# Rotating images by 180 degrees on one core: a 2 KB strip in place of a 1 KB strip ahead of the first long store

## The chip, the cores and the metric

The kernel runs on one core of a Trainium2 chip. The metric is the device time of one execution in microseconds (us); the kernel before takes 122.12 us, the median of three runs (122.01, 122.12 and 122.31).

## The reference: what is computed

The input is 32 x 3 = 96 images of 256 x 256 float32. Each is turned by 180 degrees, so its 65,536 elements come out in reversed order. Nothing is calculated; 25.17 MB are read from HBM and 25.17 MB are written.

```python
def reference(x):
    return np.rot90(x, k=2, axes=(-2, -1)).astype(np.float32)
```

## The kernel before

**Tiling.** The 96 images are three groups of 32. An image is cut into four quarters, so that a group fills 128 partitions with one row of E = 16,384 elements (64 KB) each. The three groups have a buffer each in SBUF: `A`, `Bt` and `Ct`. To reverse an image, each quarter is reversed in its own row, in place, and the quarters change places: the store (L50) writes partition quarter 3 to quarter 0 of the image and so on, through the view `[:, ::-1, lo:hi]` of the output. A store of columns `lo:hi` therefore writes 128 contiguous pieces, one a row.

**Loads.** Three loads (L47), one for each group, are issued at the start: `A` and `Ct` from SP, which feeds the DMA queue called q1 in the profile, and `Bt` from ACT, which feeds q10. Each load is 128 rows of 64 KB. The memset of `Bt` (L62) puts a small wait ahead of the load of `Bt`. A DMA is shared out over 16 DMA engines, eight rows to each.

**Turning.** VectorE (DVE) does all of the reversing with copies (the helper `copy`, L44). `swap(t, lo, w)` exchanges `w` columns from the left of a row with the mirrored `w` columns from the right, both reversed, by three copies: right part into the scratch tile `T`, left part into the right part, `T` into the left part. `turn(t, lo, hi)` covers a stretch of the left half by swaps of at most J = 2048 columns; a whole buffer is `turn(t, 0, 8192)`, four swaps. The helper keeps these copies in program order.

**Order of the work.** After the load of `A`, DVE turns three of the four swaps of `A` (columns 0 to 6144 and their mirrors). The first of these swaps makes the columns 0 to 2047 final, and a first narrow store, here called the strip, sends columns 0 to `LEAD` = 256 of each row (1 KB a row, 128 KB in all). Then DVE turns `MID` = 2560 columns of `Bt` (a swap of 2048 and one of 512), and only then the fourth swap of `A`. That fourth swap releases the long store of `A`: columns 256 to 16,384 (63 KB a row), here called the long part. The rest of `Bt` follows (5632 columns in swaps of 2048, 2048 and 1536), its store, then `Ct` and its store. All stores are issued by SP, in this order, and so stand in q1 behind the loads of `A` and `Ct`.

The part of the code that sets this order:

```python
    turn(A, 0, half - J)
    store(A, 0, 0, LEAD)
    turn(Bt, 0, MID)
    turn(A, half - J, half)
    store(A, 0, LEAD, E)
    turn(Bt, MID, half)
    store(Bt, 1, 0, E)
```

Of the kernel before, what the change touches and what calls it, by code (L numbers as in the profile page):

```python
# [2 lines left out]

os.environ.setdefault("NEURON_RT_ULTRASERVER_MODE", "4")

# [4 lines left out]


@with_exitstack
def kernel(
    ctx: ExitStack,
    tc: tile.TileContext,
    x: bass.AP,
    out: bass.AP,
):
    nc = tc.nc  # L20
    P = 128

    B, C, H, W = x.shape
    L = H * W
    G = 32
    E = L // 4
    J = E // 8

    x4 = x.rearrange("b c h w -> (b c) (h w)").rearrange(
        "(g n) (s e) -> g (n s) e", n=G, s=4)  # L30
    o4 = out.rearrange("b c h w -> (b c) (h w)").rearrange(
        "(g n) (s e) -> g n s e", n=G, s=4)

    pool = ctx.enter_context(tc.tile_pool(name="slots", bufs=1))
    A = pool.tile([P, E], x.dtype, tag="A")
    Bt = pool.tile([P, E], x.dtype, tag="B")
    Ct = pool.tile([P, E], x.dtype, tag="C")
    T = pool.tile([P, J], x.dtype, tag="T")

    def back(t, lo, hi):  # L40
        return t[:, hi - 1:(lo - 1 if lo else None):-1]

    def copy(dst, src):
        tc.keep_in_program_order(nc.vector.tensor_copy(out=dst, in_=src))  # L44

    def load(t, g, lo, hi, queue=nc.sync):
        return queue.dma_start(out=t[:, lo:hi], in_=x4[g][:, lo:hi])  # L47

    def store(t, g, lo, hi):
        return nc.sync.dma_start(  # L50
            out=o4[g][:, ::-1, lo:hi], in_=t[:, lo:hi])

    def swap(t, lo, w):
        hi = E - lo - w
        copy(T[:, 0:w], back(t, hi, hi + w))
        copy(t[:, hi:hi + w], back(t, lo, lo + w))
        copy(t[:, lo:lo + w], T[:, 0:w])

    MID = 2560
    LEAD = 256  # L60
    load(A, 0, 0, E)
    nc.vector.memset(Bt[:, 0:256], 0.0)  # L62
    load(Bt, 1, 0, E, nc.scalar)
    load(Ct, 2, 0, E)

    def turn(t, lo, hi):
        while lo < hi:
            w = min(J, hi - lo)
            swap(t, lo, w)
            lo += w  # L70

    half = E // 2
# [7 lines that stand above are left out]
    turn(Ct, 0, half)  # L80
    store(Ct, 2, 0, E)


# [1 line left out]
_INS = ['x']  # L85
_OUTS = [((32, 3, 256, 256), 'float32')]


# [23 lines left out]
```

## Time and profile before

| what | value |
|---|---|
| median of the runs (lowest to highest) | 122.12 us (122.01 to 122.31) |
| the profiled execution, its own time | 122.04 us |
| its span, first to last instruction | 120.3 us |
| VectorE busy | 44.9 us (37%), 40 instructions |
| bytes moved, rate over the span | 50.33 MB, 419 GB/s |
| load of `A`: issue, until landed | 0.73 us, 38.8 us |
| load of `Bt` | 1.16 us, 43.2 us |
| load of `Ct` | 1.18 us, 60.2 us |
| strip of `A` (128 KB): issue, until landed | 43.33 us, 18.5 us |
| long part of `A` (8064 KB) | 59.85 us, 21.0 us |
| store of `Bt` | 70.40 us, 29.8 us |
| store of `Ct` | 85.54 us, 33.9 us |

Times inside the profile are microseconds from the start of the span. The profiled execution took 1.7 us more than its span, which lies around the first and last instruction. A transfer that is issued stands in its queue until each of the 16 DMA engines has come to it; the time until it has landed therefore holds the waiting as well. The profile records every packet of the DMA engines with its queue, size, start and duration; here a packet is one row's piece of a transfer (64 KB of a load, 1 KB of the strip, 63 KB of the long part) or a 4-byte completion. In the stretches of the windows view, a packet is counted, with all of its duration and bytes, in the stretch in which it starts, so that the DMA share of a short stretch can be over 1.

### The profile page before, as it was taken

The numbers are of one execution on the slowest core, as the hardware profiler recorded it, in microseconds if no ns is written. First come the engines' busy times: TensorE is split into PE (matmuls) and PEld (weight loads), VectorE is DVE, ScalarE is ACT, GpSimd is POOL, SyncE is SP. The second block draws the span as 40 slices with busy tenths as digits, with TensorE's granted clock in tenths as the row PEclk, the third lists the DMA queues.
The fourth block names the chain that finished last, engine by engine and source line by source line (L and its number), as shares of the span: only waits on it lengthen the run. The fifth ranks groups of instructions, "written<-read, shape, count | busy, mean of one in ns | idle before, by whom it ended". The sixth has DMA issues, their size and how long they took to land.

```text
span 120.3 us, 97 instructions
## 1 busy us (share of the span) xinstructions
DVE 44.9 (37%) x40; POOL 0.2 (0%) x4
## 2 busy tenths in 40 slices
DVE  0000000000000899999999999999400000000000
POOL 0000000000000000000000000000000000000000
DMA  9888988898889988998899977988898889888990
GB/s 349 349 349 371 676 349 349 349 676 371 349 349 632 414 349 349 632 414 349 349 387 622 408 343 343 687 349 349 349 698 349 349 349 676 371 349 349 654 392 0
DMA packets 1008, 50.33 MB, mean 419 GB/s; under 512 B 112, under 2 KB 240, under 8 KB 240
## 3 DMA queue, kind: packets, MB, share of 16 engines
q1 hardware_dynamic: 864, 41.94, 81.3%
q10 hardware_dynamic: 144, 8.39, 16.1%
HBM read 25.17 MB, written 25.17 MB: 419 GB/s over the span
## 4 chain that ended last, share of the span: by engine, by line
DVE 37%; DMA 32%; issue 1%
DMA A<-in_x_dram 32%; DVE T L44 12%; DVE Bt L44 9%; DVE A L44 8%; DVE Ct L44 8%
## 5 line engine op out<-in xcount | busy, mean ns | idle before, releaser
L44 DVE COPY T<-A 128x2048 f32<-128x2048 f32 x4 | 4.9, 1227 | 38.5 <-DMA A<-in_x_dram 38.4
L44 DVE COPY Bt<-Bt 128x2048 f32<-128x2048 f32 (+2 forms) x5 | 5.1, 1013 | 0.2
L44 DVE COPY T<-Bt 128x2048 f32<-128x2048 f32 (+2 forms) x5 | 5.1, 1013 | 0.2
L44 DVE COPY Bt<-T 128x2048 f32<-128x2048 f32 (+2 forms) x5 | 5.1, 1013 | 0.2
L44 DVE COPY A<-T 128x2048 f32<-128x2048 f32 x4 | 4.9, 1227 | 0.1
L44 DVE COPY A<-A 128x2048 f32<-128x2048 f32 x4 | 4.9, 1227 | 0.1
L44 DVE COPY T<-Ct 128x2048 f32<-128x2048 f32 x4 | 4.9, 1227 | 0.1
L44 DVE COPY Ct<-T 128x2048 f32<-128x2048 f32 x4 | 4.9, 1227 | 0.1
L44 DVE COPY Ct<-Ct 128x2048 f32<-128x2048 f32 x4 | 4.9, 1226 | 0.1
L62 DVE MEMSET Bt<- 128x256 f32 x1 | 0.3, 272 | 0.9 <-PEq L96 0.9
L96 POOL MEMSET const-bfloat16-1.0<- 128x1 bf16 x1 | 0.1, 103 | 0.0
L96 POOL MEMSET const-uint8-127<- 128x1 uint8 x1 | 0.1, 102 | 0.0
L96 POOL MEMSET const-float32-0.0<- 128x1 f32 x1 | 0.1, 99 | 0.2 <-issue 0.2
L96 POOL MEMSET const-float32-1.0<- 128x1 f32 x1 | 0.1, 99 | 0.0
## 6 DMA issues: line engine op xcount, KB each, us to landing
out_dram<-A SPq DMA_DIRECT2D x1, 8064.0 KB, 21.0
out_dram<-A SPq DMA_DIRECT2D x1, 128.0 KB, 18.5
A<-in_x_dram SPq DMA_DIRECT2D x1, 38.8
Bt<-in_x_dram ACTq DMA_DIRECT2D x1, 43.2
Ct<-in_x_dram SPq DMA_DIRECT2D x1, 60.2
out_dram<-Bt SPq DMA_DIRECT2D x1, 29.8
out_dram<-Ct SPq DMA_DIRECT2D x1, 33.9
```

The lines of the kernel that those rows point to most:

```text
L44: tc.keep_in_program_order(nc.vector.tensor_copy(out=dst, in_=src))
L62: nc.vector.memset(Bt[:, 0:256], 0.0)
L96: nc = _bacc.Bacc("TRN2", target_bir_lowering=False, num_devices=1)
```

## The change

Two constants change. The strip becomes 512 columns (2 KB a row, 256 KB in all) and the long part begins at column 512 (62 KB a row). `Bt` is turned for 2432 columns, not 2560, ahead of the fourth swap of `A`: its second swap is 384 columns wide in place of 512. After the long part is issued, 5760 columns of `Bt` are left, in swaps of 2048, 2048 and 1664. The number, kind and order of the instructions on each engine stay as they were: VectorE has three copies of 384 columns in place of three of 512, and three of 1664 in place of three of 1536; SP issues the same seven transfers, two of them with another width.

```diff
-    MID = 2560
-    LEAD = 256
+    MID = 2432
+    LEAD = 512
```

## The prediction

> **What bounds the kernel.** I read the page first: span, engines, DMA packets, queues.
>
> ```profile
> span 120.3 us, 97 instructions
> ...
> DVE 44.9 (37%) x40; POOL 0.2 (0%) x4
> ...
> DMA packets 1008, 50.33 MB, mean 419 GB/s; under 512 B 112, under 2 KB 240, under 8 KB 240
> ...
> q1 hardware_dynamic: 864, 41.94, 81.3%
> q10 hardware_dynamic: 144, 8.39, 16.1%
> ```
>
> VectorE is busy for 37% of the span. The packets of the two queues together took 97.4% of the time of 16 DMA engines, which is 117.2 us for each. By the packet records the first packets start at 1.75 to 2.41 us (mean 1.93) and the last end at 118.89 to 119.13 us (mean 119.03): 117.1 us lie between. So, but for some tenths of a microsecond, the DMA engines never stop. The kernel is bound by moving 50.33 MB, and a change of order can only win what the engines lose on the way.
>
> Next the queue's own waits on SP, then the timeline around the change.
>
> ```profile
> SPq L50 <- DVE A L44: 19.6, 2, 15.9
> SPq L107 <- DMA out_dram<-Ct: 19.3, 1, 19.3
> ```
>
> ```profile
> 58.60 1.23 DVE L44 COPY A<-T 128x2048 f32<-128x2048 f32 x1
> 59.85 0.54 SPq L50 DMA_DIRECT2D out_dram<-A  x1
> 59.86 1.23 DVE L44 COPY T<-Bt 128x2048 f32<-128x2048 f32 x1
> ```
>
> The end (L107) waits for the store of `Ct`, which was issued at 85.54 us and landed 33.9 us later: it stood in its queue. The one store that is issued close to the moment at which it is needed is the long part of `A`, at 59.85 us, just as the load of `Ct` runs out. Only there can the change act. So I cut the span into stretches at the starts of the rows (columns: length, VectorE, POOL, clock, DMA share, GB/s).
>
> ```profile
> 55.46:57.88 2.42, 2.32 (x4) 0.00 (x0) 1.00 1.00 433
> 57.88:60.30 2.42, 2.35 (x3) 0.00 (x0) 1.00 1.06 433
> 60.30:60.81 0.51, 0.51 (x1) 0.00 (x0) 1.00 0.33 115
> 60.81:61.05 0.24, 0.24 (x1) 0.00 (x0) 1.00 0.49 162
> 61.05:61.20 0.15, 0.12 (x2) 0.00 (x0) 1.00 10.44 4424
> 61.20:61.48 0.28, 0.28 (x1) 0.00 (x0) 1.00 3.35 1437
> ```
>
> The first stretch holds the 16 packets of the last but one row of `Ct`: share 1.00, 2.42 us each. The second holds the 16 packets of its last row: 6% longer, 2.57 us on the mean. The strip follows. No row of the long part starts before 61.05; then 4424 GB/s for 0.15 us is 664 KB, ten rows of 64,512 bytes and some strip packets, and the last stretch holds the other six rows. Ten engines starting together means that they had waited for the transfer to arrive, 1.2 us after its issue. The packet records, put together engine by engine, say it exactly (us; lengthening is against 2.42):
>
> ```
> engines      last Ct row ends  lengthened by  strip ends     long part starts  idle
> first ten    60.45 to 60.68    0.00 to 0.20   60.80 to 61.02  61.06 to 61.14   0.11 to 0.26
> other six    60.87 to 61.13    0.17 to 0.27   61.21 to 61.47  61.22 to 61.48   0.00
> ```
>
> The strip takes 0.34 us on an engine, eight packets 0.043 us apart. Ten engines idle; six go from strip to long part at once, and these are the last. The order holds to the end: the engine that starts the long part last, at 61.476, runs its rows in 2.380 us each (later 2.418) without a pause and ends at 119.13, last of all. I call it the **pacing engine**. The earlier ones run rows of 2.380 to 2.39 and close up: the spread of 0.38 us after the first long row is 0.24 at the end.
>
> **The change, part by part.**
>
> *The strip.* A 1 KB packet costs 0.0425 us; at the rate of the long rows (64,512 bytes in 2.380 us, 27.1 bytes a ns) its bytes are 0.0378, so 0.0047 is the packet's own cost. A 2 KB packet is then 0.0756 + 0.0047 = 0.080, and eight are 0.64 us, +0.30 on each engine. Bounds: 0.60 if the own cost goes, 0.68 if it doubles with the size. I take 0.64, since only the bytes grow.
>
> *The long part.* Its rows are 1,024 bytes shorter: 8 x 0.0378 = -0.30 us on each engine. With the strip that is 0.00 on the pacing engine (bounds -0.04 and +0.04).
>
> *The swaps of `Bt`.* A copy of 512 columns takes 0.427 us, of 1536 0.960: 0.52 ns a column. A 384-column copy is then 0.360. Three of them save 3 x 0.067 = 0.20 us ahead of the fourth swap of `A`, so the long part is issued at 59.65 and reaches the engines at 60.86. The three copies of 1664 columns cost 1.027 each, +0.20, so the store of `Bt` is issued at 70.40 as before. It is needed at 80.15, when the first engine ends its long rows: 9.7 us of cover. `Ct`'s store has 99.5 - 85.5 = 14 us. The strip's issue on SP (43.33) stays; SP has nothing else before 59.65. No wait is added.
>
> *The idle time.* The first engine will now end its strip at 60.455 + 0.64 = 61.10, and the long part is there at 60.86. All ten idle stretches go, 1.56 us in sum, 0.10 us on the mean over 16 engines, and perhaps the 0.04 us by which the first long row was longer on these ten (2.42 against 2.38). The wider strip alone just covers it (61.10 against 61.06); the narrower swap gives 0.2 us of margin. But it is the engines ahead of the pacing engine that gain. The pacing engine had no idle time: 0.00.
>
> *The last row of `Ct`.* It is longer by up to 0.27 us where the load meets the strip, by 0.24 on the pacing engine (2.660). The next longest rows where one transfer meets another are 2.433 (long part to `Bt`), so this belongs to the passage from load to store. Nothing in the trace tells how it grows with the size of the strip. Bounds: it goes (-0.24), or it doubles with the strip's bytes (+0.24); and since the long part now arrives at 60.86, before six engines have ended their last `Ct` row, it may add as much again (+0.48). I take 0.00, the value of the one row there is.
>
> **Sum:** 0.00 on the pacing engine, so 122.04 for the profiled execution, which is 0.08 below the median of the runs, and 122.1 for the median. Everything that the pacing engine loses after its first row is 0.24 and 8 x 0.0047 = 0.04: no reordering here can win more than about 0.3 us, unless the engines share their rate.
>
> **The rivals.**
>
> *The store crowds the end of the load (slower).* If the lengthening of the last `Ct` row comes from store bytes that already stand in the queue, the change puts twice as many there, and the long part before the loads have ended. For it: the lengthening is only there, the strip was queued from 43.9 us on, and 0.27 is near the 0.30 us that 8 KB take on an engine. Against it: three engines, with the same strip behind them, had rows lengthened by under 0.01. Price: strip alone +0.24, 122.4; with the long part as well +0.48, 122.6. It decides, beyond what a measurement tells, once the pacing engine's last `Ct` row is over 0.61 us longer (now 0.24). The Trainium skill speaks on this side: the page "DMA: Bandwidth & Descriptors", section "Two DMAs through the same engine are not ordered", says that a queue's transfers are pipelined in an engine, whose read and write sides are separate. By that rule the strip can be read while the load is still being written, so that what is queued early need not wait its turn; the lengthened rows do not contradict it, and no run here shows the two sides apart.
>
> *The engines share a rate.* The early engines close up from 0.38 to 0.24 us, as if they gave way. If all of the idle time counted for the total, 0.10 to 0.13 us would be won: 122.0. If the issue of the long part set the end, 0.20 us would come straight off: 121.9. Against both: the pacing engine runs at the shortest row time, 2.380, throughout.
>
> *All gains at once (faster).* The lengthening vanishes (-0.24) and the shared idle time comes on top (-0.13): 121.7. Nothing supports both together.
>
> **How the numbers follow.** A measurement of this kernel tells about 0.3% from no change, 0.37 us. The forecast, nothing on the pacing engine, 122.1: 0.50. The strip alone crowds the load, 122.4: 0.13. Strip and long part crowd it, 122.6: 0.21. Shared rate or issue, 121.9 to 122.0: 0.09. All gains, 121.7: 0.07. So faster by over 0.3% 0.07, within 0.3% 0.50 + 0.13 + 0.09 = 0.72, slower 0.21. The range leaves out the last gain and the upper half of the crowding: 121.8 to 122.6.
>
> **What would show it.** In the profile after, the long part should be issued at about 59.65; the first engines should start it at about 61.10, each right behind its strip, spread over some 0.6 us instead of ten at once; the strip should take 0.64 us on an engine; and the stretch of `Ct`'s last row should keep a share of about 1.06. A share near 1.12 or above speaks for crowding, 1.00 for the lost lengthening. The last packets should end near 119.1, with a spread wider than 0.24, as the early engines win what the last one does not. The forecast is wrong if the last engine to start the long part is more than 0.3 us later or earlier, counted without the strip's 0.30, than 61.48, or if long rows change from 27.1 bytes a ns.

## The result, and the profile after

The changed kernel takes 122.27 us (median of 22 runs, 122.06 to 122.67), the kernel before 122.04 us beside it (22 runs). The ratio is 1.0022, with a 95% interval of 1.0014 to 1.0029: slower by 0.22%, some 0.25 us. The profiled execution took 122.29 us with a span of 120.5, against 122.04 and 120.3.

The page of the kernel after: as much work of VectorE, as many packets, and the strip's 128 packets are no longer under 2 KB.

```profile
span 120.5 us, 97 instructions
...
DVE 44.9 (37%) x40; POOL 0.2 (0%) x4
...
DMA packets 1008, 50.33 MB, mean 418 GB/s; under 512 B 112, under 2 KB 112, under 8 KB 240
```

The timeline of the kernel after shows the 384-column copies and the sooner issue of the long part.

```profile
55.02 0.36 DVE L44 COPY Bt<-Bt 128x384 f32<-128x384 f32 x1
...
58.33 1.23 DVE L44 COPY A<-T 128x2048 f32<-128x2048 f32 x1
59.58 0.55 SPq L50 DMA_DIRECT2D out_dram<-A  x1
```

Here are the stretches of the kernel after, cut at its own starts of rows (columns: length, VectorE, POOL, clock, DMA share, GB/s).

```profile
55.59:58.01 2.42, 2.35 (x3) 0.00 (x0) 1.00 1.00 433
58.01:60.43 2.42, 2.35 (x3) 0.00 (x0) 1.00 1.13 433
60.74:61.38 0.64, 0.61 (x2) 0.00 (x0) 1.00 0.79 301
61.38:61.60 0.22, 0.22 (x1) 0.00 (x0) 1.00 7.94 3407
61.60:62.02 0.42, 0.42 (x1) 0.00 (x0) 1.00 1.86 800
63.72:66.06 2.34, 2.27 (x3) 0.00 (x0) 1.00 1.00 434
```

The first two hold the same two rows of `Ct` as the pair shown for the kernel before. The last but one row is the same, 1.00. The last row has gone from 1.06 to 1.13: its 16 packets take 2.73 us on the mean, against 2.56. The next stretch has strip packets alone. The long part starts between 61.38 and 62.02, eleven rows in the fourth stretch (3407 GB/s for 0.22 us is 750 KB) and five in the fifth, as each engine comes to the end of its strip; nothing is idle. The prediction had named this share as its sign: 1.12 or above for crowding, 1.00 for a lengthening that is lost. The packet records carry no number of the engine; packets are joined into 16 chains where one starts within 0.01 us of the end of another, and across idle time in the order of time. This is the chain of the pacing engine in both kernels:

```
pacing engine            before    after     difference
last Ct row starts       58.469    58.453    -0.02
it takes                  2.660     2.912    +0.25
strip, with completion    0.347     0.648    +0.30
long part starts         61.476    62.013    +0.54
8 long rows of            2.380     2.342    -0.30
last packet ends        119.134   119.371    +0.24
```

The whole difference, 0.24 us at the last packet and 0.25 in the time, is the last row of `Ct`. Strip and long rows cancel.

### The profile page after: what moved, and what is told of

It reads as the page before. It is cut to its first block, busy times and chain, and to the rows that moved or that the text cites. A ratio compares the mean times of both kernels' runs of the same rounds, so it can differ in the third digit from the quotient of the medians.

```text
span 120.5 us, 97 instructions
## 1 busy us (share of the span) xinstructions
DVE 44.9 (37%) x40; POOL 0.2 (0%) x4
## 4 chain that ended last, share of the span: by engine, by line
DVE 37%; DMA 32%; issue 1%
DMA A<-in_x_dram 32%; DVE T L44 12%; DVE Bt L44 9%; DVE A L44 8%; DVE Ct L44 8%
## 6 DMA issues: line engine op xcount, KB each, us to landing
out_dram<-A SPq DMA_DIRECT2D x1, 256.0 KB, 19.1
```

## The experiments

The theory: **bytes that a later transfer is to read from SBUF, standing in the queue behind the load of `Ct`, lengthen the load's last row.** The expectations call it Q where they speak of store bytes, and R where they add that these are read from SBUF ahead of their turn. Rivals: the sooner long part does it (L), the passage from load to store does it whatever is queued (P), the width of the strip costs by itself, the writes to HBM do it (W), or any further transfer does (S). The table has one line for each run. "Row" is the mean packet of the last `Ct` row (without lengthening it is 2.418 to 2.422), "long" the start of the long part, or of the whole store of `A`, on the last engine, "end" the end of the last packet; these are of one profiled execution each. Ratios are to the kernel before, with 95% intervals.

```
strip, columns of Bt         ratio                     row    long    end
1 KB, 2560 (before)          1                         2.557  61.48  119.13
the same, profiled again     one time, 121.97 us       2.517  61.39  119.06
2 KB, 2432 (after)           1.0022 [1.0014, 1.0029]   2.733  62.01  119.37
2 KB, 2560                   1.0021 [1.0005, 1.0037]   2.856  61.97  119.33
2 KB, 2560, moved in code    1.0037 [1.0022, 1.0052]   2.838  62.06  119.42
1 KB, 2432                   0.9994 [0.9980, 1.0007]   2.460  61.28  118.94
1 KB, 2432, again            0.9987 [0.9975, 1.0000]   2.459  61.26  118.92
none, 2560                   1.0030 [1.0020, 1.0040]   2.418  61.42  119.59
8 KB, 2560                   1.0066 [1.0047, 1.0085]   3.633  64.73  120.28
load in its place, 2560      1.0039 [1.0024, 1.0054]   2.440  61.56  119.52
copy in SBUF, 2560           1.0077 [1.0055, 1.0099]   2.696  62.29  120.25
none, 0                      1.0081 [1.0063, 1.0099]   3.324  61.96  119.92
2 KB issued after, 2560      1.0034 [1.0022, 1.0045]   2.421  61.95  119.52
none, 2304                   1.0004 [0.9995, 1.0014]   2.420  61.15  119.34
1 KB, 2304                   0.9988 [0.9976, 0.9999]   2.496  61.33  118.98
512 B, 2304                  0.9989 [0.9980, 0.9999]   2.443  61.12  119.03
2 KB, 2304                   1.0026 [1.0010, 1.0041]   2.740  61.85  119.21
```

### The change taken apart

The wider strip alone:

```diff
-    LEAD = 256
+    LEAD = 512
```

> The strip is 2 KB a row, the first part of Bt stays at 2560 columns. Theory Q (store bytes that already stand in the queue behind the load of Ct lengthen its last row, in proportion to their number): the mean packet of the last Ct row is about 2.75 us, as in the changed kernel (2.42 without lengthening, 2.57 with the 1 KB strip), and the time is 0.2 to 0.3 us above the kernel before. Theory L (the long part, arriving 0.2 us sooner, lengthens the row): the mean packet stays at 2.57 us and the time within 0.05 us of the kernel before.

```profile
57.80:60.22 2.42, 2.35 (x3) 0.00 (x0) 1.00 1.18 433
```

Slower by 0.21%, row 2.856, a share of 1.18 (1.06 in the kernel before). The strip alone brings the whole loss. The row was expected at 2.75; it is 0.1 us longer than that.

The narrower swap alone:

```diff
-    MID = 2560
+    MID = 2432
```

> The strip stays at 1 KB a row, 2432 columns of Bt are turned ahead of the fourth swap of A, so that the long part is issued at 59.65 us. Theory Q: the last Ct row keeps a mean packet of 2.57 us, the idle stretches of the ten early engines shrink by 0.2 us each, and the time stays within 0.05 us of the kernel before, since the last engine had none. Theory L: mean packet about 2.75 us and 0.2 to 0.3 us slower.

```profile
57.80:60.22 2.42, 2.35 (x3) 0.00 (x0) 1.00 1.02 433
```

The ratio of 0.9994 leaves no loss to it, and the row is not longer but a little shorter. Theory L falls. The pacing engine gained, though it had no idle time: its last row was 2.432 against 2.660.

### How the last row depends on the strip

No strip (the first `store` call is taken out):

```diff
-    LEAD = 256
+    LEAD = 0
...
-    store(A, 0, 0, LEAD)
```

> No strip: the whole store of A (64 KB a row) is issued where the long part was, at 59.85 us. Theory Q: the last Ct row is not lengthened at all, its mean packet is 2.42 us; the engines end it at about 60.3 to 60.9 and idle until the store arrives at 61.06, start together, and the time is within 0.1 us of the kernel before, since what is won on the row is lost in the wait. A third theory, P (the lengthening belongs to the passage from load to store, whatever is queued): 2.57 us for the packet again, and the time within 0.1 us too.

With nothing behind the load the row is 2.418 on the mean, and no engine is over 2.420. P falls. The stretches of this kernel:

```profile
57.97:60.39 2.42, 2.35 (x3) 0.00 (x0) 1.00 1.00 433
60.39:61.25 0.86, 0.84 (x1) 0.00 (x0) 1.00 0.01 0
61.25:61.45 0.20, 0.18 (x1) 0.00 (x0) 1.00 12.27 5243
```

The last `Ct` row has a share of 1.00; then nothing but completions starts until 61.25, and all 16 rows of the store start within 0.2 us. The time missed the expectation: 0.30% above, not within 0.1 us. The last engine ended its `Ct` row at 61.06 and waited 0.35 us. And the 24 rows that followed took it 58.17 us, against 57.96 for the same 24 rows in the kernel with no strip and no columns of `Bt`, whose engines start between 61.29 and 61.96. The expectation had set the wait equal to the 0.24 us won on the row, and had left out the slower rows.

A strip of 8 KB:

```diff
-    LEAD = 256
+    LEAD = 2048
```

> The strip is 2048 columns, 8 KB a row, 64 KB on each engine, eight times that of the kernel before. Theory Q without a limit: the last Ct row of the last engine is 8 x 0.24 = 1.9 us longer than 2.42, and the kernel 1.7 us slower than before. Theory Q with a limit to what an engine takes up ahead: more than the 0.49 us of the 2 KB strip, less than 1.9 us, and the time above before by that less 0.24 us. Theory L: 0.24 us as before, and the same time.

```profile
57.80:60.22 2.42, 2.35 (x3) 0.00 (x0) 1.00 1.50 433
```

That stretch of the 8 KB kernel has a share of 1.50: row 3.633, on the last engine 3.598, 1.18 us longer. That is far from eight times 0.24; the growth is not in proportion.

The whole store queued early (strip taken out, and the fourth swap of `A` ahead of all of `Bt`):

```diff
-    MID = 2560
-    LEAD = 256
+    MID = 0
+    LEAD = 0
...
-    store(A, 0, 0, LEAD)
```

> No strip, and no part of Bt is turned ahead of the fourth swap of A: the whole store of A, 64 KB a row, is issued at about 54.7 us and stands in the queue when the load of Ct ends. Theory Q, by the 8 KB strip (64 KB on each engine, mean row 3.63 us): the last Ct row takes 3.6 us or more, no engine idles, and the time is about 0.9 us above the kernel before. If only packets of a strip, of 8 KB and less, do it, the row stays at 2.42 us, the stores follow at once, and the time is 0.2 to 0.3 us below the kernel before.

```profile
57.80:60.22 2.42, 2.35 (x3) 0.00 (x0) 1.00 1.37 433
```

The store was issued at 54.64 us and stood in the queue; the row took 3.324 on the mean (up to 3.70), and the kernel is 0.81% slower with no engine idle. A packet of 64 KB does it as well as small ones. The row is shorter than behind the 8 KB strip, though 3.6 us or more was expected and eight times as many bytes stood in the queue when the row began, so the lengthening has a limit. The run also shows what the work order of the kernel before is good for: it keeps the long part out of the queue until the loads end.

### Width, or standing in the queue

First the strip was moved in the code behind the fourth swap, with 512 columns:

```diff
-    store(A, 0, 0, LEAD)
     turn(Bt, 0, MID)
     turn(A, half - J, half)
+    store(A, 0, 0, LEAD)
     store(A, 0, LEAD, E)
```

> The 2 KB strip is issued by SP only with the long part, at 59.85 us, in place of 43.3 us, so that it reaches the DMA engines (1.2 us later, 61.06) after the load of Ct has ended. Theory Q (store bytes that stand in the queue behind the load lengthen its last row): the last Ct row goes back to 2.42 us with the same strip, the last engine starts its long part at about 61.06 + 0.64 = 61.7 us against 62.01 in the changed kernel, and the time is within 0.1 us of the kernel before, 0.2 to 0.3 us below the changed one. Rival, the width of the strip by itself (2 KB packets) costs: the time stays 0.2 to 0.3 us above the kernel before.

This did not do what it was meant to: the timeline has the strip on SP at 43.39 us as ever (the line below takes the first two stores of `A` together), since it waits only for the columns that it reads, and these are final after the first swap. So it is a second look at the 2 KB strip with 2560 columns (row 2.838), and says nothing on the rival.

```profile
43.39 17.07 SPq L50 DMA_DIRECT2D out_dram<-A  x2
```

Then the first swap of `A` itself was put last:

```diff
-    LEAD = 256
+    LEAD = 512
...
-    turn(A, 0, half - J)
-    store(A, 0, 0, LEAD)
+    turn(A, J, half)
     turn(Bt, 0, MID)
-    turn(A, half - J, half)
+    turn(A, 0, J)
+    store(A, 0, 0, LEAD)
     store(A, 0, LEAD, E)
```

> The first swap of A is turned last, after the 2560 columns of Bt, so that the 2 KB strip cannot be issued before 59.85 us, together with the long part, and reaches the DMA engines at about 61.06, after the load of Ct has ended. Theory R (store bytes in the queue behind the load are read from SBUF ahead of their turn and lengthen its last row): the last Ct row takes 2.42 us, though the strip is as wide as in the changed kernel; the last engine starts its long part at about 61.75 us against 62.01, and the time is 0.2 to 0.3 us below the changed kernel, within 0.1 us of the kernel before. Rival, the wider strip costs by its width alone: 0.2 us or more above the kernel before, with a last Ct row of 2.7 us.

Now the timeline has both stores on SP, one after the other, from 59.83 us, and the stretch of the last row is clean:

```profile
59.83 1.27 SPq L50 DMA_DIRECT2D out_dram<-A  x2
```

```profile
57.80:60.22 2.42, 2.35 (x3) 0.00 (x0) 1.00 1.00 433
```

The same 2 KB strip no longer lengthens the row (2.421, at most 2.449). Width is not the cause; standing in the queue behind the load is. The time did not fall with it: 0.34% above, where 0.0 was expected. The first strip packet starts at 61.115, 1.28 us after the issue, while the last engine had ended its load at 60.92; it starts its long part at 61.95, and the rows from there to the end take 57.57 us against 57.36 in the changed kernel. What the row won, the wait and the slower rows gave back.

### What kind of transfer does it

A load of the same size in the strip's place, into an unused tile, with `LEAD = 0`:

```diff
+    U = pool.tile([P, 512], x.dtype, tag="U")
...
-    store(A, 0, 0, LEAD)
+    nc.sync.dma_start(out=U, in_=x4[0][:, 0:512])
```

> The store strip is replaced by a load of the same size (2 KB of each row of the input into an unused tile), queued behind the load of Ct; the whole store of A is issued at 59.85 us. It moves 0.26 MB more than the kernel before. Theory R (the engine reads the strip from SBUF ahead of its turn, while it still writes the last load row into SBUF) and theory W (writes of the strip to HBM meet the last reads from HBM): the last Ct row stays at 2.42 us, the extra load takes 0.64 us on an engine, the last one starts its store at about 61.55, and the time is about 0.35 us above the kernel before. Theory S (any further transfer in the queue lengthens the row): 2.73 us or more for that row, and 0.6 to 0.8 us above.

```profile
57.80:60.22 2.42, 2.35 (x3) 0.00 (x0) 1.00 1.01 433
```

Row 2.440: three engines took 2.51 to 2.56, the others 2.418 to 2.420. The kernel is 0.39% slower, 0.47 us, where about 0.35 was expected for the extra 0.26 MB. A further transfer as such does not lengthen the row to 2.73; S falls.

A copy of the strip's columns from SBUF to SBUF, again with `LEAD = 0`:

```diff
+    U = pool.tile([P, 512], x.dtype, tag="U")
...
-    store(A, 0, 0, LEAD)
+    nc.sync.dma_start(out=U, in_=A[:, 0:512])
```

> The store strip is replaced by a copy of the same columns from A in SBUF to an unused tile in SBUF, issued where the strip was; the whole store of A is issued at 59.85 us. It moves 0.26 MB more inside SBUF. Theory R: the last Ct row is lengthened as by the 2 KB strip, to a mean of 2.7 to 2.9 us, though nothing is written to HBM, and the time is 0.6 to 0.9 us above the kernel before. Theory W: 2.42 us for the row, since the copy writes nothing to HBM, and about 0.35 us above.

```profile
57.80:60.22 2.42, 2.35 (x3) 0.00 (x0) 1.00 1.11 433
```

The copy writes nothing to HBM, and the row is lengthened all the same: 2.696, on every engine by 0.09 us or more, at most to 2.906. W is not needed. Load and copy both write 2 KB a row into SBUF from the same place in the queue; only the copy reads it from SBUF. The ratio is 1.0077 against 1.0039. So, between these two, the lengthening comes with the queued read of SBUF. One difference is left in the pair: the extra load waits for nothing and was issued at once, the copy when the first swap had ended. The pages give the time from issue to landing, 60.3 and 19.1 us:

```profile
U<-in_x_dram SPq DMA_DIRECT2D x1, 256.0 KB, 60.3
...
U<-A SPq DMA_DIRECT2D x1, 256.0 KB, 19.1
```

A load that is issued as late as the copy was not run. Of the 0.73 us by which the last packets of the two executions differ, 0.49 is the last row on the last engine; the rest is that this row began 0.24 us later.

The traces bound the theory in two ways. In the changed kernel the store of `Bt`, which also reads SBUF, is issued 9.8 us before the first engine ends its long rows, yet the eighth long row takes 2.342 us on every engine like the seven before it: behind this store there is no lengthening. And in the kernel with the extra load, the last engine writes its 2 KB rows from 60.92 to 61.56 us, while the store reaches the first engines at 61.12; these packets take 0.084 us throughout. So what was seen is the lengthening of a 64 KB load row; for short packets, behind which the store has only just come, none was seen.

### The sooner long part, and a better version

> The kernel before, profiled once more, to see how far the lengthening of the last Ct row differs from one execution to the next. Expected: a mean packet of 2.50 to 2.62 us (2.56 at first), the first ten or so engines idle for 0.1 to 0.25 us ahead of the long part, and 122.0 us.

Row 2.517, 121.97 us; here thirteen engines idle ahead of the long part, for 0.02 to 0.14 us, and again the last three do not. Expected were about ten engines with 0.1 to 0.25 us.

> The same kernel as the narrower swap alone (strip 1 KB, 2432 columns), run again, for its time and for a second look at the last Ct row. If the mean packet of 2.46 us, against 2.56 in the kernel before, comes from the sooner arrival of the long part, it stays near 2.46 and the time 0.1 us below the kernel before; if it was chance, it lies anywhere between 2.45 and 2.65, and the time is within 0.05 us of the kernel before.

Row 2.459 again, ratio 0.9987 with an interval that just reaches 1.

Four kernels with `MID = 2304` followed, with no strip and with strips of 1 KB, 512 bytes and 2 KB:

```diff
-    MID = 2560
-    LEAD = 256
+    MID = 2304
+    LEAD = 0
...
-    store(A, 0, 0, LEAD)
```

> No strip, and 2304 columns of Bt ahead of the fourth swap of A: the whole store of A is issued at about 59.45 us and reaches the engines at 60.66, while the last rows of Ct end at 60.3 to 60.9. Theory R: early engines idle for at most 0.3 us, the last ones have a row lengthened by at most some tenths, and the time is 0.2 to 0.4 us below that of the kernel with no strip and 2560 columns, so about that of the kernel before (0.0 to 0.1 us above). Were the wait for the store not the cost there, the time would stay 0.4 us above the kernel before.

As expected: 0.33 us less than with no strip and 2560 columns (122.13 against 122.46), with the row still at 2.420. The wait for the store was most of the cost there: on the last engine it went from 0.35 to 0.10 us.

```diff
-    MID = 2560
+    MID = 2304
```

> The strip of the kernel before (1 KB) and 2304 columns of Bt, so that the long part is issued 0.40 us sooner than before, at about 59.45 us, and reaches the engines at 60.66, while most last rows of Ct (60.4 to 61.0) are still being written. If the sooner long part shortens the last Ct row (2.46 us on the mean at 2432 columns in both looks, 2.52 and 2.56 at 2560), it is 2.40 to 2.46 here and the time 0.1 to 0.2 us below the kernel before. If store bytes in the queue lengthen it, as theory R says, the long part's bytes now do, the mean is over 2.6 us, and the time 0.0 to 0.3 us above the kernel before.

```diff
-    MID = 2560
-    LEAD = 256
+    MID = 2304
+    LEAD = 128
```

> A strip of 512 bytes a row, and 2304 columns of Bt (long part at about 59.45 us). Theory R: the strip alone would lengthen the last Ct row by some 0.07 us on the mean (0.14 with 1 KB), the strip takes about 0.19 us on an engine, so most engines end it near the 60.66 us at which the long part arrives; the time is 0.1 to 0.2 us below the kernel before, as with the 1 KB strip and 2432 columns. If the wait for the long part or its bytes cost more than that, the time is at or above that of the kernel before.

```diff
-    MID = 2560
-    LEAD = 256
+    MID = 2304
+    LEAD = 512
```

> The changed kernel with 2304 columns of Bt in place of 2432: the 2 KB strip and a long part issued at about 59.45 us. If the sooner long part shortens the last Ct row also behind a 2 KB strip (2.73 us at 2432 columns, 2.84 and 2.86 at 2560), it is about 2.6 us here and the time 0.1 us below the changed kernel. If it does not (no reason is known why it should), the mean is 2.7 us or more and the time that of the changed kernel or 0.1 us above it.

With the 1 KB strip the row is 2.50, ratio 0.9988; with 512 bytes 2.44, ratio 0.9989; with 2 KB 2.74, 0.26% slower. With 1 KB that is neither of the two rows expected (2.40 to 2.46, or over 2.6). The sooner issue goes along with a shorter row by 0.06 to 0.12 us between 2560 and 2432 columns, in one or two profiled executions each, for both widths of strip (2.46, 2.46 against 2.52, 2.56; 2.73 against 2.84, 2.86), and a further 128 columns bring nothing more (2.50; 2.74). Why a sooner long part should shorten the row is not settled: the theory would have it longer. The best versions are the kernel before with 2432 or 2304 columns, about 0.1 us faster (121.9 against 122.05), at the edge of what the runs can tell.

## Why the prediction was wrong

**Right.** *The bound*: the DMA engines stay busy, and only the passage from load to store changed. *The pacing engine*: the engine that starts the long part last ended last in both kernels, and the end moved with it (+0.54 at the start of the long part, -0.30 in its rows, +0.24 at the end). *The strip*: forecast 0.64 us, measured 0.644 (0.648 with its completion). *The long part*: rows of 2.342 us, as forecast. *The swaps*: copies of 0.360 us as forecast, long part issued at 59.58 (59.65 forecast; this execution's first store was 0.07 sooner as well), `Bt`'s store at 70.33 with its cover whole. *The idle time*: all ten idle stretches are gone, and the pacing engine, which had none, won nothing by it. The spread of the last packets is 0.62 us, wider than 0.24, as forecast.

**Wrong, one step: "The last row of `Ct`" - "I take 0.00, the value of the one row there is."** It was +0.25 us on the pacing engine (2.660 to 2.912) and +0.18 on the mean. The first engine started its long part at 61.39 instead of 61.10: 0.16 us of that is its longer last row, and 0.13 that this row began later in this execution. The bound set beside it, +0.24 if it doubles with the strip's bytes, is what came; the rival "The store crowds the end of the load" had the mechanism, and its price for the strip alone, +0.24 us, the loss. It had been put behind for three engines whose rows were not lengthened. That was one look at something that differs from engine to engine and from look to look: behind a 1 KB strip the pacing engine's row was longer by 0.24, 0.01, 0.22, 0.29 and 0.01 us in five executions, behind 2 KB by 0.49, 0.58, 0.55 and 0.51 in four. Three rows out of 16 that escape do not speak against a cause which acts on the mean. That the pacing engine's row doubled so exactly is therefore partly luck. The second half of the rival's price (0.24 more from the long part) did not come: the narrower swap cost nothing.

The doubling is not a law either. The mean lengthening was 0.02 us with 512 bytes a row, 0.04 to 0.14 with 1 KB, 0.31 to 0.44 with 2 KB, 1.21 with 8 KB, 0.91 with a queued 64 KB row. The Trainium skill, page "DMA: Bandwidth & Descriptors", section "Two DMAs through the same engine are not ordered", has the read and the write side of an engine as separate queues. The pair of load and copy agrees with a read side that takes up the next transfer's SBUF reads while the row is still being written (2.440 against 2.696); that it happens inside the engine, and not on the way to SBUF, no run here shows.

The +0.22% lies within the range given for the time, but the forecast was no change, and the rival that the numbers follow had been given 0.13. The prediction's limit for being wrong, 0.3 us at the start of the last engine's long part, was too wide to notice: without the strip's 0.30 that start moved by 0.24.

## What to carry to other kernels

Where a load and a store follow each other in one DMA queue, do not queue more of the store behind the load than is needed to bridge the time until the rest arrives: in this kernel 512 bytes to 1 KB a row was enough, 2 KB cost 0.25 us and the whole store 0.9 to 1.0 us. This was seen behind a load; behind a store, in the same traces, it was not. Look for the engine that ends last before pricing idle time on the others. And where a single duration is unexplained and the change doubles something next to it, the doubled value belongs in the forecast, not only in the range.

## What was not expected of the hardware

DMA engines that had waited for a store, and so start its rows nearly together, run them a little slower. With no strip and 2560 columns all 16 had waited and started within 0.2 us; their first rows took 2.45 to 2.46 us, and the last engine's 24 rows 58.17 us in all. With the store queued early none had waited: every row took 2.418 us, and the same 24 rows 57.96. Starting together is not enough for it. In that kernel three engines started within 0.008 us of one another and ran at 2.418 all the same. In the changed kernel, where none waits either, three started within 0.006 us, and every engine had every long row at 2.342 and every later row at 2.418. In the kernel with the extra load, the three engines that had come to its end before the store arrived had first rows of 2.45 to 2.46, and 12 of the 13 others 2.418. This was compared between kernels and engines, not varied by itself, and why a wait should have this effect is open.
